# A decoder block on one core: 14 of 22 input-projection slabs by Strassen's seven products in a first phase

## Chip, core and metric

The kernel runs on one core of a Trainium2 chip. The metric is the device time of one execution in microseconds (us). Shown are the median of three runs and one further execution that was profiled.

## What is computed

The reference is one decoder block for 1024 tokens of width 1024: a norm, one input projection whose columns feed a gated linear attention (GLA), a retention and two merging gates, an output projection, and a mixture of 32 experts. All matrices are float32. Cut to what matters here:

```
u    = rmsnorm(x)                                # 1024 x 1024
proj = u @ w_in                                  # 1024 x 11280
gq, gk, gv, gg, gdown, rq, rk, rv, rg, mga, mgb = split(proj)
#512 512 1024 1024 16 1024 1024 2048 2048 1024 1024 columns
o_gla = rmsnorm(gla(gq, gk, gv, decay(gdown))) * silu(gg)
o_ret = groupnorm(retention(rotary(rq), rotary(rk), rv)) * silu(rg)
merged = sigmoid(mga) * (o_gla @ w_br_gla) + sigmoid(mgb) * (o_ret @ w_br_ret)
h = x + merged @ w_out
out = rmsnorm(h + moe(rmsnorm(h)))
```

Without the 16 columns of gdown the projection is 22 slabs of 512 columns: gq 1, gk 1, gv 2, gg 2, rq 2, rk 2, rv 4, rg 4, mga 2, mgb 2.

## The kernel before

**Arithmetic.** A float32 operand is split in two parts, hi and lo (`split`, L139: ScalarE casts to hi, VectorE subtracts to get lo). A product takes three matmuls, hi·hi, hi·lo, lo·hi (`Acc.add`, L154 to L157); each brings its own 128x128 stationary operand. Loading a weight slab of 1 MB and splitting it is `load_w` (L159): one DMA on SP's queue, two casts and two subtractions of 128x1024. Raw slabs have two buffers (`wraw`), split slabs two (`wsp`), and PSUM has eight banks.

**Order.** The tokens are done in two halves of 512, `Half(0)` and then `Half(1)`, and each half reads and splits all of w_in. `feat` (L323) makes 128 output columns as rows of a bank: 8 blocks of k by 3 matmuls, 24 in all, weights stationary and 512 tokens moving. `toks` (L331) makes 4 banks of 128 tokens by 512 columns: 96 matmuls for 1024 k, tokens stationary and 512 weight columns moving. So a 512-column slab costs 96 matmuls of 128x512 per half either way.

A half's program is a hand-written list (`seq`, `middle`, L1010 to L1130): norm and transposes of x (`start_x`, L304, `turn_x`), the decay's input, the gates mga and mgb (`gate`, L341, stored in DRAM), then GLA in two pairs of heads: `gq`, `gk`, `gv`, `gg`, the scores (`gs`), and four chunks (`gc`) that hand on a state. `gla_exact` (`gx`, L486) is a branch that is not taken here. After it come the norm of the GLA output (`gn`, L545), its transposes (`gt`, L559) and its projection (`gy`). The retention follows, head by head: `rk`, `rq` (two `feat` and a rotary on VectorE, L620), `rv`, `rg` (`toks`), `rkt`, scores (`rs`, L653), state (`rst`), output (`ro`, L724), its transposes (`rt`, L752) and its projection (`ry`, L764). The part of the list for head h with p = h - 1 reads

```
do(half, f"rk{h}", f"ro{p}", f"rq{h}", f"rt{p}", f"rv{h}0", f"rv{h}1", f"ry{p}0", f"ry{p}1")
```

so that the two `toks` calls of rv stand between the transposes of the previous head and its projection. The compiler layer turns the list into a fixed order for each engine; it may put an instruction that is ready ahead of one that isn't, with the list's order as priority, but it does not move work across the branch of `gx`. In the run each engine works its own order strictly.

The expert stage begins at about 1633 us and is untouched.

Of the kernel before, what the change touches and what calls it, by code (L numbers as in the profile page):

```python
# [28 lines left out]
SEQ = 1024  # L29
# [15 lines left out]
SPARE = 32  # L45
# [45 lines left out]
def hybrid_block(tc, a, out, dbg=None):  # L91
# [13 lines left out]
    sm_d = [tc.dram_tile([128, 8, HALF], F32, name=f"sm{i}_d") for i in range(2)]  # L105
# [13 lines left out]
    rsm = top.enter_context(tc.tile_pool(name="rsm", bufs=1))  # L119
# [39 lines left out]
    def load_w(src, kt, n, swap=False):  # L159

        raw = wraw.tile([128, kt, n], F32, name="w_raw", tag="w_raw")
        SP.dma_start(raw, src)
        if swap:
# [15 lines left out]
    upool = top.enter_context(tc.tile_pool(name="upool", bufs=4))  # L179
    mixers = contextlib.ExitStack()  # L180
    trig = mixers.enter_context(tc.tile_pool(name="trig", bufs=1))
    slots = mixers.enter_context(tc.tile_pool(name="slots", bufs=NSLOT))
    mixs = mixers.enter_context(tc.tile_pool(name="mixs", bufs=2))

    def slot(shape=(128, 512), dt=F32):
        return slots.tile(list(shape), dt, name="slot", tag="slot")

    x0 = [[slot(), slot()] for t in range(4)]
# [44 lines left out]

    s_gla = consts.tile([128, 4, 256], F32, name="s_gla")
    E_all = consts.tile([128, 2, 8, 32], F32, name="E_all")
    rk_all = consts.tile([128, 8, 2], F32, name="rk_all")

    rows_v = consts.tile([128, 8, 2, 2], F32, name="rows_v")
    DVE.tensor_copy(rows_v[:, :, :, 0], desth)
    DVE.tensor_copy(rows_v[:, :, :, 1], destl)  # L240
    wts_v = consts.tile([128, 8, 2, 3], BF16, name="wts_v")
    rows_b = consts.tile([128, 8, 2, 2, 32], BF16, name="rows_b")
    wts_b = consts.tile([128, 8, 2, 3, 32], BF16, name="wts_b")
    avs = consts.tile([128, 8, 2, CAP], BF16, name="avs")
# [20 lines left out]
    class Half:  # L265
# [8 lines left out]
        def load_x(self):  # L274
            if self.half == 0:
                self.xn = x0
                return
# [53 lines left out]
        def toks(self, w, part, accs):  # L331

            if part == 0:
                accs[:] = [Acc(bank(), 8) for t in range(4)]
            for t in range(4):
                for k in range(4):
                    s = slice(128 * t, 128 * t + 128)
                    accs[t].add(self.uh[4 * part + k][:, s], self.ul[4 * part + k][:, s], w[0][:, k, :], w[1][:, k, :])


        def gate(self, w, i, c, keep=False):  # L341
            for j in range(2):
                ps = self.feat(w, 128 * j)
                s = slot()
# [3 lines left out]
                else:  # L348
                    SP.dma_start(sm_d[i][:, 2 * c + j, :], s)
# [55 lines left out]
        def gla_q(self, w, pair):  # L405
            self.qt = []
            for j in range(2):
                ps = self.feat(w, 128 * j)
                q = self.ep[2 * pair + j]
                DVE.scalar_tensor_tensor(q, ps, 128.0 ** -0.5, q, op0=OP.mult, op1=OP.mult)  # L410
                self.qt.append(q)

        def gla_k(self, w, pair):
            self.kt = []
            for j in range(2):
                ps = self.feat(w, 128 * j)
                k = self.en[2 * pair + j]
                DVE.tensor_mul(k, ps, k)
                self.kt.append(k)

        def gla_v(self, w, part):
            if part == 0:
                self.accs = []
            self.toks(w, part, self.accs)
            if part == 1:
                self.v = []
                for t in range(4):
                    s = slot((128, 2, 256))
                    ACT.copy(s.rearrange("p j d -> p (j d)"), self.accs[t].ps)
                    self.v.append(s)  # L430

        def gla_g(self, w, part, pair):
            if part == 0:
                self.accs = []
            self.toks(w, part, self.accs)
            if part == 1:
                self.gg = getattr(self, "gg", {})
                for t in range(4):
                    s = slot((128, 2, 256))
                    ACT.activation(s.rearrange("p j d -> p (j d)"), self.accs[t].ps, AF.Silu)  # L440
                    self.gg[pair, t] = s

        def gla_scores(self):
            self.sc, self.kk = [], []
            for j in range(2):
                q, k = self.qt[j], self.kt[j]
# [13 lines left out]
        def gla_chunk(self, c, pair):  # L460
# [7 lines left out]
            for j in range(2):  # L468
                h = 2 * pair + j
                vc = self.v[c][:, j, :]  # L470
                PE.matmul(po[:, j, :], self.sc[j][:, c, :], vc, start=True, stop=first)
                if not first:
                    PE.matmul(po[:, j, :], self.qt[j][:, 128 * c:128 * c + 128], s_gla[:, h, :], start=False, stop=True)
# [98 lines left out]
        def gla_y(self, w, c):  # L572

            for j in range(2):
                s = slot()
                SP.dma_start(s, sm_d[0][:, 2 * c + j, :])
# [43 lines left out]
        def rotary(self, w):  # L620

            pe, po = self.feat(w, 0), self.feat(w, 128)
# [11 lines left out]
        def ret_k(self, w):  # L634
            self.kr = self.rotary(w)

        def ret_q(self, w):
# [38 lines left out]
        def ret_v(self, w, part, h):  # L676
            if part == 0:
                self.accs = []
            self.toks(w, part, self.accs)
            if part == 1:  # L680
                self.vh = [slot(dt=F32R) for _ in range(4)]
                self.vl = [slot(dt=F32R) for _ in range(4)]
                for t in range(4):
                    split(self.vh[t], self.vl[t], self.accs[t].ps, gneg[:, h, t:t + 1])

        def ret_g(self, w, part, h):
            if part == 0:
                self.accs = []
            self.toks(w, part, self.accs)
            if part == 1:  # L690
                self.sg = [slot() for _ in range(4)]
                for t in range(4):
                    ACT.activation(self.sg[t], self.accs[t].ps, AF.Silu)
# [94 lines left out]
        def load_m(self):  # L788
            self.mg, self.mh, self.ml = [], [], []
            for f in range(8):  # L790
# [3 lines left out]
                if g is None:  # L794
                    g = slot()
                    SP.dma_start(g, sm_d[1][:, f, :])
# [153 lines left out]


# [24 lines left out]
    gix = consts.tile([CAP, 32], I32, name="gix")  # L976
    swt = consts.tile([CAP, 32], F32, name="swt")

# [20 lines left out]
    prog = []  # L999

    def add(fn, *args, spec=None):
        prog.append((spec, fn, args))
# [4 lines left out]
    def s512(w, off, part):  # L1007
        return (w[:, 4 * part:4 * part + 4, off:off + 512], 4, 512, False)

    def seq(z):  # L1010
# [7 lines left out]
        put("start", z.start_x)  # L1018
# [7 lines left out]
        for i, off in enumerate((OFF_MA, OFF_MB)):  # L1026
            for c in range(4):
                put(f"gate{4 * i + c}", z.gate, i, c, z.half == 1 and 4 * i + c == 7, spec=s256(off + 256 * c))
        for p in range(2):
            put(f"gq{p}", z.gla_q, p, spec=s256(OFF_GQ + 256 * p))  # L1030
            put(f"gk{p}", z.gla_k, p, spec=s256(OFF_GK + 256 * p))
            for part in range(2):
                put(f"gv{p}", z.gla_v, part, spec=s512(w_in, OFF_GV + 512 * p, part))
                put(f"gg{p}", z.gla_g, part, p, spec=s512(w_in, OFF_GG + 512 * p, part))
            put(f"gs{p}", z.gla_scores)
# [9 lines left out]
        for h in range(4):  # L1045
            put(f"rk{h}", z.ret_k, spec=s256(OFF_RK + 256 * h, True))
            put(f"rq{h}", z.ret_q, spec=s256(OFF_RQ + 256 * h, True))
            for part in range(2):
                put(f"rv{h}{part}", z.ret_v, part, h, spec=s512(w_in, OFF_RV + 512 * h, part))
                put(f"rg{h}{part}", z.ret_g, part, h, spec=s512(w_in, OFF_RG + 512 * h, part))  # L1050
# [23 lines left out]
    def middle(half, mix):  # L1074

        def at(n):
# [3 lines left out]
        do(half, "gq0", "gk0", "gv0")  # L1080
        at("gs0")
        do(half, "gs0", "gc00", "gg0", "gc01", "gc02", "gc03", "gq1", "gk1", "gv1", "gs1",
           "gc10", "gg1", "gc11", "gc12", "gc13", "gx", "gn0", "rk0", "gn1")
        at("gt0")
        do(half, "gt0", "gt1", "gy0", "gy1", "gy2", "gy3", "rq0")
        for h in range(4):
            p = h - 1
            if h:
                do(half, f"rk{h}", f"ro{p}", f"rq{h}", f"rt{p}", f"rv{h}0", f"rv{h}1", f"ry{p}0", f"ry{p}1")
                if half == 0:  # L1090
                    do(half, f"rkt{h}")
            elif half == 0:
                do(half, "rv00", "rkt0", "rv01")
# [313 lines left out]
```

## Time and profile before

| | us |
|---|---|
| median of 3 runs | 2281.86 (2277.16 to 2282.0) |
| profiled execution, its time | 2281.08 |
| its span, first to last instruction | 2279.1 |
| TensorE matmul busy | 2177.4 (96%) |
| VectorE busy | 1311.9 (58%) |
| ScalarE busy | 1083.0 (48%) |

In the views an instruction is named by line, engine, operation and `out<-in`; `bank<-w_hi,uh` is a matmul into PSUM with w_hi moving and uh stationary. PE is TensorE, PEld its weight loads, DVE VectorE, ACT ScalarE. Matmuls overlap in their pipeline, so what one costs is the distance between starts and not its duration.

### The profile page before, as it was taken

Reading aid. Unit: us, or ns where it says so; the run is one execution under the profiler, and the core shown is the slowest. Engines: PE = TensorE matmul, PEld = TensorE weight load, DVE = VectorE, ACT = ScalarE, POOL = GpSimd, SP = SyncE. Lnnn points to the kernel's source line nnn. Section 1 sums busy time; section 2 is a strip of 40 time slices with the busy share of each in tenths; the row PEclk is TensorE's granted clock in tenths of the full one; section 3 lists DMA queues with packets and bytes.
Section 4 is the critical chain, followed back from the end, with each engine's and each line's share of the span. In section 5 each row is a group of like instructions: output and inputs, shape, how many; then the busy total and the mean of one; then the engine's idle time right before and its main releaser. Section 6 shows DMA issues by size and latency. Waiting matters only on the chain. (4 is left out here: it accounts for less than half of the span.)

```text
span 2279.1 us, 25815 instructions
## 1 busy us (share of the span) xinstructions
PE 2177.4 (96%) x9950; PEld 1765.5 (77%) x9951; DVE 1311.9 (58%) x2015; ACT 1083.0 (48%) x1504; POOL 145.5 (6%) x116
## 2 busy tenths in 40 slices
PE   6999999999999999999999999999599999999993
PEld 5888788888888888887888888878467777777772
DVE  5522354525356628334445354535588888888886
ACT  5522433333334437323233332333377888888885
POOL 1000000000000011000000000001311111111102
PEclk9999999999999999999999999999799999999996
DMA  5432242222223544222422222237489999998995
GB/s 166 144 115 74 85 155 95 84 93 83 99 77 111 202 146 164 95 74 77 175 96 70 93 76 100 74 120 277 174 315 324 368 370 370 371 369 312 369 364 201
DMA packets 157953, 406.16 MB, mean 178 GB/s; under 512 B 13887, under 2 KB 65119, under 8 KB 133488
## 3 DMA queue, kind: packets, MB, share of 16 engines
q1 hardware_dynamic: 149088, 387.01, 47.4%
q0 software_dynamic: 8720, 17.28, 3.2%
q8 instruction: 83, 1.36, 0.2%
q14 instruction: 62, 0.51, 0.1%
HBM read 372.97 MB, written 44.04 MB: 183 GB/s over the span
## 5 line engine op out<-in xcount | busy, mean ns | idle before, releaser
L142 ACT CAST w_hi<-w_raw 128x1024 fp32r<-128x1024 f32 (+1 forms) x244 | 247.8, 1052 | 559.8 <-PE bank L156 488.8
L143 DVE TENSOR_TENSOR w_lo<-w_raw,w_hi 128x1024 fp32r<-128x1024 f32 (+1 forms) x244 | 293.3, 1225 | 365.6 <-ACT w_hi L142 347.1
L143 DVE TENSOR_TENSOR m_lo<-m_raw,m_hi 128x1024 fp32r<-128x1024 f32 x380 | 445.1, 1219 | 66.7 <-ACT m_hi L142 64.4
L142 ACT CAST m_hi<-m_raw 128x1024 fp32r<-128x1024 f32 x380 | 381.8, 1050 | 68.0 <-PE bank L156 63.8
L156 PE MATMUL bank<-w_hi,uh 128*128 128x512 f32 x768 | 300.7, 392 | 0.0
L156 PE MATMUL bank<-w_lo,uh 128*128 128x512 f32 x768 | 299.3, 390 | 0.0
L156 PE MATMUL bank<-w_hi,ul 128*128 128x512 f32 x768 | 299.2, 390 | 0.0
L156 PE MATMUL bank<-uh,w_hi 128*128 128x512 f32 x656 | 261.5, 399 | 7.9 <-ACT junk L256 4.0
L156 PE MATMUL bank<-ul,w_hi 128*128 128x512 f32 x656 | 259.9, 396 | 0.0
L156 PE MATMUL bank<-uh,w_lo 128*128 128x512 f32 x656 | 259.3, 395 | 0.0
L156 PE MATMUL bank<-slot,w_hi 128*128 128x512 f32 x768 | 237.0, 390 | 1.1 <-DVE slot L146 0.9
L156 PE MATMUL bank<-m_lo,xh 128*112 128x512 f32 x512 | 206.8, 404 | 0.7 <-DVE m_lo L143 0.2
L156 PE MATMUL bank<-m_hi,xh 128*112 128x512 f32 x512 | 204.8, 400 | 1.9 <-ACT xh L142 1.6
L156 PE MATMUL bank<-m_hi,xl 128*112 128x512 f32 x512 | 202.6, 396 | 0.0
L156 PEld LDWEIGHTS bank<-slot,w_hi 128*128 128x128 f32 x768 | 144.0, 188 | 32.0 <-DVE slot L146 1.7
L156 PEld LDWEIGHTS bank<-w_hi,ul 128*128 128x128 f32 x768 | 144.2, 188 | 30.1
L156 PEld LDWEIGHTS bank<-w_hi,uh 128*128 128x128 f32 x768 | 144.3, 188 | 29.4
L156 PEld LDWEIGHTS bank<-w_lo,uh 128*128 128x128 f32 x768 | 144.3, 188 | 29.3
L156 PEld LDWEIGHTS bank<-uh,w_hi 128*128 128x128 f32 x656 | 125.9, 192 | 38.2 <-ACT junk L256 4.4
L156 PE MATMUL bank<-slot,w_lo 128*128 128x512 f32 x384 | 149.1, 390 | 0.0
L156 PEld LDWEIGHTS bank<-uh,w_lo 128*128 128x128 f32 x656 | 125.6, 191 | 26.7 <-issue 0.3
L156 PEld LDWEIGHTS bank<-ul,w_hi 128*128 128x128 f32 x656 | 125.9, 192 | 25.9
(264 smaller groups left out, 2890.7 us busy)
## 6 DMA issues: line engine op xcount, KB each, us to landing
w_raw<-in_w_in_dram SPq DMA_DIRECT2D x88, 1024.0 KB, 4.7
m_raw<-in_expert_w_down_dram SPq DMA_DIRECT2D x64, 1024.0 KB, 12.9
m_raw<-in_expert_w_gate_dram SPq DMA_DIRECT2D x63, 1024.0 KB, 13.3
m_raw<-in_expert_w_up_dram SPq DMA_DIRECT2D x63, 1024.0 KB, 12.7
w_raw<-in_w_branch_ret_dram SPq DMA_DIRECT2D x16, 1024.0 KB, 4.8
slot<-in_x_dram SPq DMA_DIRECT2D x32, 256.0 KB, 6.0
w_raw<-in_w_branch_gla_dram SPq DMA_DIRECT2D x8, 1024.0 KB, 4.9
w_raw<-in_w_out_dram SPq DMA_DIRECT2D x8, 1024.0 KB, 5.8
```

Source lines behind the costliest of these rows:

```text
L142: ACT.copy(hi, src)
L143: DVE.tensor_sub(lo, src, hi.bitcast(F32))
L156: PE.matmul(self.ps, l, r, start=self.i == 0, stop=self.i == 3 * self.n - 1)
```

## The change

A class `Front` runs ahead of the two halves. It takes 14 slabs (mga 2, gv 2, gg 2, rv 4, rg 4) for all 1024 tokens at once. With tokens, k and columns each cut in two, a slab is a 2x2 by 2x2 block product of eight products of 512 tokens by 512 k by 256 columns; the Winograd form of Strassen's scheme needs seven, with sums of the left blocks (S1 to S4, made once), sums of the right blocks (per slab) and sums of the results. The products run in the order a11, s2, a12, s3, s1, a22, s4 (left blocks and sums); `pair` makes and splits their right sums, two at a time, a pair ahead. `turn` transposes the second half's x and makes S1 and S2, `third` and `fourth` make S3 and S4 with two VectorE sums and a split for each of four k blocks. Results go to DRAM (silu and sigmoid applied), and the halves load them back where they computed them before. The weights of these slabs are read once and not twice. The other eight slabs stay in the halves; their calls are cut in two (`gq0a`, `gq0b`, ...). The order lists are rewritten.

```diff
+        def product(self, feat, left, right):
+            (lh, ll), (rh, rl) = left, right
+            banks = [bank(), bank()]
+            for j in range(2):
+                for t in range(1 if feat else 2):
+                    acc = Acc(banks[j] if feat else banks[j][:, 256 * t:256 * t + 256], 4)
+                    for k in range(4):
+                        if feat:
+                            s = slice(128 * j, 128 * j + 128)
+                            acc.add(rh[:, k, s], rl[:, k, s], lh[k], ll[k])
+                        else:
+                            s = slice(256 * j + 128 * t, 256 * j + 128 * t + 128)
+                            acc.add(lh[k][:, s], ll[k][:, s], rh[:, k, :], rl[:, k, :])
+            return banks
+        def pair(self, z, i):
+            (b11, b12), (b21, b22) = ((r[:, :, :256], r[:, :, 256:]) for r in z["raw"])
+            if i == 0:
+                z["x"] = x = fl.tile([128, 4, 256], F32, name="x_raw")
+                DVE.tensor_sub(x, b22, b12)
+                DVE.tensor_sub(b12, b12, b11)
+                r = self.rights(2)
+                split(*r[0], b11)
+                DVE.tensor_add(b11, b11, x)
+                split(*r[1], b11)
+            elif i == 1:
+                r = self.rights(2)
+                split(*r[0], b21)
+                split(*r[1], z["x"])
...
+        def slab(self, z, r, then):
+            nxt = then(0)
+            ps = self.product(feat, self.a11, r[0])
+            p1 = [fs.tile([128, HALF], F32, name="fs", tag="fs") for j in range(2)]
+            for j in range(2):
+                ACT.copy(p1[j], ps[j])
+            ps = self.product(feat, self.s2, r[1])
+            u2 = [self.room() for j in range(2)]
+            for j in range(2):
+                DVE.tensor_add(u2[j], ps[j], p1[j])
...
+        def turn(self, k):
...
+            ACT.activation(r3, ps[0], AF.Copy, scale=nmix[:, k:k + 1])
+            DVE.scalar_tensor_tensor(r1, ps[1], nmix[:, k + 4:k + 5], r3, op0=OP.mult, op1=OP.add)
+            split(self.a22[0][k], self.a22[1][k], ps[1], nmix[:, k + 4:k + 5])
+            DVE.tensor_sub(r2, r1, h11)
+            DVE.tensor_sub(r2, r2, l11)
+            split(self.s2[0][k], self.s2[1][k], r2)
+            split(self.s1[0][k], self.s1[1][k], r1)
...
+    H[0].start_x()
+    H[0].gate(w, 1, 0, early=True)
+    for t in range(4):
+        H[1].norm_x(t)
+    for k in range(4):
+        fr.turn(k)
+    H[0].gate(w, 1, 1, early=True)
+    r0 = fr.pair(z0, 0)
+    for k in range(4):
+        fr.third(k)
+    for k in range(4):
+        fr.fourth(k)
+    fr.run(pieces, r0, z0)
+        def rows_of(self, src, c0):
+            res = [slot() for t in range(4)]
+            for t in range(4):
+                r0 = self.tok0 + 128 * t
+                SP.dma_start(res[t], src[r0:r0 + 128, c0:c0 + 512])
+            return res
-        do(half, "gs0", "gc00", "gg0", "gc01", "gc02", "gc03", "gq1", "gk1", "gv1", "gs1",
-           "gc10", "gg1", "gc11", "gc12", "gc13", "gx", "gn0", "rk0", "gn1")
+        do(half, "gs0", "gq1a", "gc00", "gq1b", "gc01", "gv1", "gk1a", "gc02", "gk1b", "gc03", "gs1", "gg0",
+           "rk0a", "gc10", "rk0b", "gc11", "rq0a", "gc12", "rq0b", "gc13", "gg1", "gx", "gn0", "gn1")
         at("gt0")
-        do(half, "gt0", "gt1", "gy0", "gy1", "gy2", "gy3", "rq0")
+        do(half, "gt0", "gt1", "rv0", "gy0", "gy1", "gy2", "gy3")
-                do(half, f"rk{h}", f"ro{p}", f"rq{h}", f"rt{p}", f"rv{h}0", f"rv{h}1", f"ry{p}0", f"ry{p}1")
+                do(half, f"rk{h}a", f"rk{h}b", f"ro{p}", f"rv{h}", f"rq{h}a", f"rq{h}b", f"rt{p}", f"ry{p}0", f"ry{p}1")
...
+            do(half, f"rvs{h}", f"rs{h}", f"rg{h}")
...
-    middle(0, {"gt0": [(0, ["gate7"])], "rg30": [(1, ["x"])], "rg31": [(1, ["norm0", "norm1"])], "rst3": [(1, ["norm2", "norm3"])]})
+    middle(0, {"gt0": [(0, ["gate3"])], "rst3": [(1, ["x", "norm0", "norm1", "norm2", "norm3"])]})
...
-    middle(1, {"gs0": [(0, ["rd"])], "gt0": [(1, ["gate6"])]})
-    do(1, "ro3", "gate7", "rt3", "lm", "ry30", "ry31", "lh", "wo00", "wo01", "th0")
+    middle(1, {"gt0": [(0, ["rd"])]})
+    do(1, "ro3", "gate3", "rt3", "lm", "ry30", "ry31", "lh", "wo00", "wo01", "th0")
```

In the new lists `gv`, `gg`, `rv` and `rg` are loads alone, and `rvs` splits the loaded rv.

## Rows read from the trace of the kernel before

**Rows 1.** The page: busy time, then TensorE and its granted clock in 40 slices.

```profile
PE 2177.4 (96%) x9950; PEld 1765.5 (77%) x9951; DVE 1311.9 (58%) x2015; ACT 1083.0 (48%) x1504; POOL 145.5 (6%) x116
...
PE   6999999999999999999999999999599999999993
...
PEclk9999999999999999999999999999799999999996
```

**Rows 2.** Who TensorE waited for: us in total, times, longest us.

```profile
PE bank L294 <- DVE slot L291: 17.2, 5, 11.4
...
PE bank L156 <- ACT junk L256: 4.0, 1, 4.0
```

**Rows 3.** Stretches of 50 us: busy TensorE, loads, VectorE, ScalarE, GpSimd, clock, DMA share.

```profile
200.00:250.00 50.00, 50.00 (x234) 41.68 (x233) 13.94 (x16) 11.81 (x15) 0.00 (x0) 1.00 0.25 85
...
1050.00:1100.00 50.00, 45.30 (x205) 36.78 (x204) 30.41 (x72) 24.87 (x55) 0.00 (x0) 0.93 0.37 124
```

**Rows 4.** TensorE in order of time: start, us; 512-wide matmuls, first and last of 44.

```profile
386.15 0.39 PE L156 MATMUL bank<-w_hi,uh 128*128 128x512 f32 x1
...
395.90 0.39 PE L156 MATMUL bank<-w_lo,uh 128*128 128x512 f32 x1
```

**Rows 5.** The same, the 256-wide matmuls of one call of `rs`, merged.

```profile
382.66 1.59 PE L156 MATMUL bank<-slot 128*128 128x256 f32 x12
```

**Rows 6.** Groups by line and shape: count, busy us, mean ns of one; TensorE, loads.

```profile
L156 PE MATMUL bank<-slot 128*128 128x256 f32 x96 | 12.7, 282 | 0.0
...
L156 PEld LDWEIGHTS bank<-w_hi,uh 128*128 128x128 f32 x768 | 144.3, 188 | 29.4
```

**Rows 7.** Groups by line and shape on VectorE and ScalarE.

```profile
L143 DVE TENSOR_TENSOR w_lo<-w_raw,w_hi 128x1024 fp32r<-128x1024 f32 x240 | 290.7, 1233 | 365.6 <-ACT w_hi L142 347.1 <-PE bank L647 8.2 <-PE bank L828 7.9
...
L777 DVE TENSOR_TENSOR yb<-yb,bank 128x512 f32<-128x512 f32 x48 | 32.7, 684 | 46.3 <-PE bank L156 46.3
...
L142 ACT CAST w_hi<-w_raw 128x1024 fp32r<-128x1024 f32 x240 | 245.5, 1059 | 558.8 <-PE bank L156 488.3 <-issue 67.3 <-ACT slot L345 1.6
```

**Rows 8.** DMA issues: KB each, median us from issue to landing.

```profile
w_raw<-in_w_in_dram SPq DMA_DIRECT2D x88, 1024.0 KB, 4.7
```

**Rows 9.** The start in order of time: TensorE and VectorE.

```profile
25.54 0.80 PE L156 MATMUL bank<-uh,w_hi 128*128 128x512 f32 x1 [0.22 <-DVE ul L146]
...
22.80 0.88 DVE L291 TENSOR_SCALAR slot<-slot,rstd 128x512 f32<-128x512 f32 x2
...
24.74 5.35 DVE L146 SCALAR_TENSOR_TENSOR ul<-bank,nmix,uh 128x512 fp32r<-128x512 f32 x8
```

**Rows 10.** TensorE in order of time: the 32 transposes of the second half's x.

```profile
735.87 3.65 PE L294 MATMUL bank<-ct,slot 128*128 128x128 f32 x32
```

**Rows 11.** After the branch of `gx`, second half: TensorE, then VectorE's first norm.

```profile
1058.63 0.77 PE L156 MATMUL bank<-uh,w_hi 128*128 128x512 f32 x1 [4.01 <-ACT junk L256]
...
1063.24 0.58 PE L156 MATMUL bank<-ul,w_hi 128*128 128x512 f32 x1
1063.65 0.39 PE L156 MATMUL bank<-uh,w_lo 128*128 128x512 f32 x1
...
1068.03 3.26 DVE L556 SCALAR_TENSOR_TENSOR slot<-slot,rstd 128x256 f32<-128x256 f32 x8
```

**Rows 12.** TensorE: one whole call of `rs`, and one of `rkt`.

```profile
380.23 4.01 PE L156 MATMUL bank<-slot 128*128 128x512 f32 x24
...
368.46 1.03 PE L647 MATMUL bank<-ct,slot 128*128 128x128 f32 x8
```

**Rows 13.** The transposes `rt` of one head, and the splits that follow them.

```profile
439.88 1.98 PE L758 MATMUL bank<-ct,slot 128*128 128x128 f32 x16
...
440.07 0.69 DVE L627 TENSOR_TENSOR slot<-bank,sin_t 128x512 f32<-128x512 f32 x1 [2.29 <-PE bank L156]
...
441.41 2.35 DVE L143 TENSOR_TENSOR w_lo<-w_raw,w_hi 128x1024 fp32r<-128x1024 f32 x2
...
447.63 2.72 DVE L146 SCALAR_TENSOR_TENSOR slot<-bank,rnw,slot 128x512 fp32r<-128x512 f32 x4
```

More of the change, by code (lines that the diff above doesn't have):

```diff
@@ L104, in hybrid_block @@
     st_d = tc.dram_tile([4, 128, 2, 512], F32, name="st_d")
-    sm_d = [tc.dram_tile([128, 8, HALF], F32, name=f"sm{i}_d") for i in range(2)]
+    sm_d = [tc.dram_tile([128, 8, SEQ], F32, name=f"sm{i}_d") for i in range(2)]
+    gv_d = tc.dram_tile([SEQ, 1024], F32, name="gv_d")
+    gg_d = tc.dram_tile([SEQ, 1024], F32, name="gg_d")
+    rv_d = tc.dram_tile([SEQ, 2048], F32, name="rv_d")
+    rg_d = tc.dram_tile([SEQ, 2048], F32, name="rg_d")
     ma_d = tc.dram_tile([128, 8, HALF], F32, name="ma_d")
@@ L162, in load_w, with split_w @@
         SP.dma_start(raw, src)
+        return split_w(raw, kt, n, swap)
+    def split_w(raw, kt, n, swap=False):
         if swap:
@@ L178, in hybrid_block, with left_sum @@
     ypool = top.enter_context(tc.tile_pool(name="ypool", bufs=8))
[L179 to L188, printed above, removed]
+    front = contextlib.ExitStack()
+    fl = front.enter_context(tc.tile_pool(name="fl", bufs=1))
+    fs = front.enter_context(tc.tile_pool(name="fs", bufs=4))
+    def left_sum(name):
+        return [fl.tile([128, 4, HALF], F32R, name=f"{name}{p}") for p in ("h", "l")]
+    s1, s2, a22 = left_sum("s1"), left_sum("s2"), left_sum("a22")
+    rows = contextlib.ExitStack()
+    fx = rows.enter_context(tc.tile_pool(name="fx", bufs=1))
+    x0, x1 = ([[fx.tile([128, HALF], F32, name=f"x{h}{t}{c}") for c in range(2)] for t in range(4)] for h in range(2))
     for c in range(2):
@@ L329, in feat, with gate @@
             return ps
[L331 to L341, printed above, removed]
+        def gate(self, w, i, c, keep=False, early=False):
             for j in range(2):
                 ps = self.feat(w, 128 * j)
-                s = slot()
+                s = fs.tile([128, HALF], F32, name="fs", tag="fs") if early else slot()
                 ACT.activation(s, ps, AF.Sigmoid)
@@ L421, in gla_v @@
[L421 to L441, printed above, removed]
@@ L443, in gla_scores, with gla_q, gla_k @@
-        def gla_scores(self):
+        def gla_q(self, w, pair, j):
+            if w is not None:
+                self.w = w
+            ps = self.feat(self.w, 128 * j)
+            q = self.ep[2 * pair + j]
+            DVE.scalar_tensor_tensor(q, ps, 128.0 ** -0.5, q, op0=OP.mult, op1=OP.mult)
+        def gla_k(self, w, pair, j):
+            if w is not None:
+                self.w = w
+            ps = self.feat(self.w, 128 * j)
+            k = self.en[2 * pair + j]
+            DVE.tensor_mul(k, ps, k)
@@ new lines, in rows_of, with gla_v, gla_g @@
+        def rows_of(self, src, c0):
[4 more added lines that the diff above has]
+            return res
+        def gla_v(self, pair):
+            self.v = getattr(self, "v", {})
+            self.v[pair] = [z.rearrange("p (j d) -> p j d", j=2) for z in self.rows_of(gv_d, 512 * pair)]
+        def gla_g(self, pair):
+            self.gg = getattr(self, "gg", {})
+            for t, z in enumerate(self.rows_of(gg_d, 512 * pair)):
+                self.gg[pair, t] = z.rearrange("p (j d) -> p j d", j=2)
@@ L469, in gla_chunk @@
                 h = 2 * pair + j
-                vc = self.v[c][:, j, :]
+                vc = self.v[pair][c][:, j, :]
                 PE.matmul(po[:, j, :], self.sc[j][:, c, :], vc, start=True, stop=first)
                 if not first:
-                    PE.matmul(po[:, j, :], self.qt[j][:, 128 * c:128 * c + 128], s_gla[:, h, :], start=False, stop=True)
+                    PE.matmul(po[:, j, :], self.ep[h][:, 128 * c:128 * c + 128], s_gla[:, h, :], start=False, stop=True)
                 if not last:
@@ L674, in ret_scores, with ret_v, ret_vs, ret_g @@
                 self.pl.append(lo)
[L676 to L693, printed above, removed]
+        def ret_v(self, h):
+            self.vr = self.rows_of(rv_d, 512 * h)
+        def ret_vs(self, h):
+            self.vh, self.vl = [], []
+            for t in range(4):
+                hi, lo = slot(dt=F32R), slot(dt=F32R)
+                split(hi, lo, self.vr[t], gneg[:, h, t:t + 1])
+                self.vh.append(hi)
+                self.vl.append(lo)
+        def ret_g(self, h):
+            self.sg = self.rows_of(rg_d, 512 * h)
         def ret_state(self, h):
@@ L998, in hybrid_block @@
     H = [Half(0), Half(1)]
-    prog = []
-    def add(fn, *args, spec=None):
-        prog.append((spec, fn, args))
+    H[0].xn = x0
     def s256(off, swap=False):
@@ L1008, in s512 @@
         return (w[:, 4 * part:4 * part + 4, off:off + 512], 4, 512, False)
+    early = []
+    for c in range(2):
+        raw = wraw.tile([128, 8, 256], F32, name="w_raw", tag="w_raw")
+        SP.dma_start(raw, s256(OFF_MB + 256 * c)[0])
+        early.append(raw)
+    for t in range(4):
+        for c in range(2):
+            SP.dma_start(x1[t][c], x_t[:, 4 + t, 512 * c:512 * c + 512])
+    H[0].start_x()
+    pieces = [(True, AF.Sigmoid, sm_d[0], OFF_MA + 512 * i, 512 * i) for i in range(2)]
@@ new lines, in hybrid_block @@
+    for dst, fn, off, n in ((gv_d, None, OFF_GV, 2), (gg_d, AF.Silu, OFF_GG, 2), (rv_d, None, OFF_RV, 4), (rg_d, AF.Silu, OFF_RG, 4)):
+        pieces += [(False, fn, dst, off + 512 * i, 512 * i) for i in range(n)]
+    fr = Front(H[0].uh, H[0].ul)
+    w = split_w(early[0], 8, 256)
+    H[0].gate(w, 1, 0, early=True)
+    H[1].xn = x1
+    for t in range(4):
+        H[1].norm_x(t)
+    w = split_w(early[1], 8, 256)
+    for k in range(4):
+        fr.turn(k)
+    H[0].gate(w, 1, 1, early=True)
@@ new lines, in hybrid_block @@
+    z0 = dict(raw=[fr.load(pieces[0][3], kh) for kh in range(2)])
+    r0 = fr.pair(z0, 0)
+    rows.close()
+    fl2 = front.enter_context(tc.tile_pool(name="fl2", bufs=1))
+    fr.s3, fr.s4 = (fr.by_k([fl2.tile([128, 4, HALF], F32R, name=f"{n}{p}") for p in ("h", "l")]) for n in ("s3", "s4"))
+    for k in range(4):
[3 more added lines that the diff above has]
+    fr.run(pieces, r0, z0)
+    front.close()
+    keep = top.enter_context(tc.tile_pool(name="keep", bufs=1))
@@ new lines, in hybrid_block, with slot @@
+    rsm = top.enter_context(tc.tile_pool(name="rsm", bufs=1))
+    mixers = contextlib.ExitStack()
+    trig = mixers.enter_context(tc.tile_pool(name="trig", bufs=1))
+    slots = mixers.enter_context(tc.tile_pool(name="slots", bufs=NSLOT))
+    mixs = mixers.enter_context(tc.tile_pool(name="mixs", bufs=2))
+    def slot(shape=(128, 512), dt=F32):
+        return slots.tile(list(shape), dt, name="slot", tag="slot")
+    s_gla = keep.tile([128, 4, 256], F32, name="s_gla")
+    E_all = keep.tile([128, 2, 8, 32], F32, name="E_all")
@@ L1010, in seq, with add @@
+    DVE.memset(base, 0.0)
+    flag_i = keep.tile([1, 2], I32, name="flag_i")
+    gix = keep.tile([CAP, 32], I32, name="gix")
+    swt = keep.tile([CAP, 32], F32, name="swt")
+    prog = []
+    def add(fn, *args, spec=None):
+        prog.append((spec, fn, args))
     def seq(z):
@@ L1025, in seq @@
             put("r" + n, getattr(z, "route_" + n))
-        for i, off in enumerate((OFF_MA, OFF_MB)):
-            for c in range(4):
-                put(f"gate{4 * i + c}", z.gate, i, c, z.half == 1 and 4 * i + c == 7, spec=s256(off + 256 * c))
+        for c in range(4):
+            put(f"gate{c}", z.gate, 1, c, z.half == 1 and c == 3, spec=s256(OFF_MB + 256 * c))
         for p in range(2):
[L1030 to L1035, printed above, removed]
+            put(f"gq{p}a", z.gla_q, p, 0, spec=s256(OFF_GQ + 256 * p))
+            put(f"gq{p}b", z.gla_q, None, p, 1)
+            put(f"gk{p}a", z.gla_k, p, 0, spec=s256(OFF_GK + 256 * p))
+            put(f"gk{p}b", z.gla_k, None, p, 1)
+            put(f"gv{p}", z.gla_v, p)
+            put(f"gg{p}", z.gla_g, p)
+            put(f"gs{p}", z.gla_scores, p)
             for c in range(4):
@@ L1045, in seq @@
         for h in range(4):
[L1046 to L1050, printed above, removed]
+            put(f"rk{h}a", z.ret_k, spec=s256(OFF_RK + 256 * h, True))
+            put(f"rk{h}b", z.ret_k)
+            put(f"rq{h}a", z.ret_q, spec=s256(OFF_RQ + 256 * h, True))
+            put(f"rq{h}b", z.ret_q)
+            put(f"rv{h}", z.ret_v, h)
+            put(f"rvs{h}", z.ret_vs, h)
+            put(f"rg{h}", z.ret_g, h)
             put(f"rkt{h}", z.ret_kturn)
@@ L1111, in hybrid_block @@
     do(1, "gate1")
-    do(0, "wo00", "wo01")
-    do(1, "gate2")
-    do(0, "th0", "wo10", "wo11")
-    do(1, "da", "gate3")
-    do(0, "th1")
-    do(1, "db", "gate4")
+    do(0, "wo00", "wo01", "wo10", "wo11")
+    do(1, "da", "gv0", "gate2")
+    do(0, "th0", "th1")
+    do(1, "db")
     do(0, "ra")
```

192 lines of the change are left out of this document (134 added, 58 removed).

## The prediction

> **What bounds the kernel now.** The page's busy times come first: TensorE 96%, VectorE 58%, ScalarE 48% of the span [rows 1]. The 40 slices show where the missing 4% lies: the first slice, the step from the projections to the experts (slice 29) and the end; in between TensorE is full at the full clock [rows 1]. A busy TensorE may still be waiting on something, so the waits come next: over the whole span the largest is 17.2 us at the start, on the norms of x, and the next is one wait of 4.0 us [rows 2]. The stretches say the same from the other side: between 200 and 250 us TensorE is busy for all 50 us, VectorE for 13.9, ScalarE for 11.8, and DMA has a share of 0.25 [rows 3]. So until 1633 us the time is the number of matmuls times their distance, and other engines matter only where TensorE waits for them.
>
> The distance is read from starts. Forty-three steps from 386.15 to 395.90 us give 226.7 ns for a 512-wide matmul [rows 4]. Twelve 256-wide ones take 1.59 us together, the last of them 282 ns, so (1.59 - 0.28) / 11 = 118.8 ns each, with a fresh stationary operand every time [rows 5, 6]. Twice 118.8 is 237.6: a narrow matmul costs 5% more per column.
>
> **The change part by part.**
>
> *Products.* Before, a slab costs 2 x 96 matmuls of 226.7 ns = 43.5 us over both halves. After, the two gate slabs take 7 x 24 = 168 of them, 38.1 us, and save 10.9 us together. The twelve token slabs take 7 x 48 = 336 narrow ones, 336 x 118.8 ns = 39.9 us, and save 3.6 us each, 43.3 us. Sum: **-54.2 us**. Strassen's eighth would be 76 us; the rest goes on the narrow form.
>
> *Right sums, splits and result sums inside the phase.* Per slab VectorE has 7 splits and 4 sums of 128x1024 at 1.23 us and 14 result sums of 0.68 us, 23 us; ScalarE has 7 casts of 1.06 us and some ten small ones, 14 us [rows 7]. Both lie beside 38 to 40 us of matmuls, and the pairs are split a pair ahead. The tightest place is the slab's end: the next slab's first right block can be cast only when a22 has released its buffer, and needs cast plus split, 2.3 us, and up to 1.4 us of result sums, while s4 covers it with 5.5 to 5.7 us. I take nothing; with that cover gone it would be about 2 us x 13.
>
> *DMA.* Weights of the 14 slabs are read once (28 MB less), results are written and read back (29 MB each way). A slab's 4 MB stand beside 39 us, and 1 MB lands in 4.7 us [rows 8]. The loads wait on SP behind the stores of results; those are ready before the next raw buffer is free. The reloads are issued well ahead of use. I take nothing. Late next, if at all, would be `gg1`, whose slots come free last.
>
> *The start.* Matmuls begin at 25.5 us as before: the first gate's weights can be split in the pauses of the norms. Behind that, VectorE owes much before TensorE can go on. From 30.1 us, when the splits of u end [rows 9]: one weight slab 2.4, four norms about 11 (13 small steps and two scalings each, 0.88 for the scalings [rows 9]), `turn` 4 x 6 x 0.68 = 16, the first pair 6.1, `third` and `fourth` 24 x 0.68 = 16, the second pair's first split 1.2: 53 us, so until 83 us. TensorE has two gates (96 x 226.7 ns = 21.8 us), 32 transposes (3.7 us [rows 10]) and two products (10.9 us) to set against it, 36 us, until 62. The gap is 21 us if VectorE works strictly in the list's order, and 13 if the second pair goes ahead of `fourth`, 8 us long. I take **+18 us**, nearer the strict order.
>
> *After `gx`.* Before, the next matmul follows 4.0 us after the last, and the chain to the first normed GLA rows ends at 1068.03 + 3.26 = 1071.3, 12.7 us after that matmul's start [rows 11]. What covers it now is `toks` work, `rk0` and a gate. After the change the first half has `gate3` (10.9 us) and the scores of head 0 (4.0 us [rows 12]) and loses nothing. The second half has only the scores: 12.7 - 4.0 = 8.7, so **+9 us**; from 6 us, if more can be put there, to 13 us.
>
> *Between `rt` and `ry`.* Here 96 matmuls of `rv`, 21.8 us, go away. The transposes end at 439.88 + 1.98 = 441.9 us, and the first of the four splits on VectorE that `ry` needs ends near 447.63 + 0.74 = 448.4: 6.5 us, because the rotary of `rq` and a weight slab stand before it on VectorE [rows 13]. Both stay there (`ry`'s second slab takes the place of `rv`'s). The place recurs for three heads in each half. TensorE may take `rs` (4.0 us) and in the first half `rkt` (1.0 us) meanwhile [rows 12], as both stand next in the list. I take 2.5 and 1.5 us, **+12 us** for the six. The ends: 1.1 us each, if the rotary were out of the way too, and 6.5 us each.
>
> *Smaller edges.* The changeover from the phase to the halves (a chain of cast and split), and `rt3` before `ry30` in the second half: +2 us each, **+4 us**; from 0 to 10. The cut of calls in two adds no instruction. The new layout of pools is taken at nothing, as it must only hold the same buffers.
>
> Sum: -54.2 + 18 + 9 + 12 + 4 = **-11 us**. The profiled execution took 2281.1 us, 0.8 under the median, so 2270 in the profile's terms and 2271 as a median.
>
> **A rule against it.** Twelve matmuls in a row with a fresh stationary operand start 118.8 ns apart although one load is 188 ns long, so loads run beside matmuls and beside each other [rows 5, 6]. The Trainium skill, "TensorE: Matmul & The Clock Gate", section "The mechanism", states that a weight load overlaps a running matmul only where their row groups differ, which none does here. By that rule the narrow form would pay 4032 loads where the wide one paid 2304; 1728 more at the trace's 188 ns are an estimate of +325 us on the sum above, 2596 us. The trace contradicts it over a run of twelve; a milder form of it is rival C.
>
> **Rivals.**
>
> *A, the waits stay open: slower.* For A speaks that each engine's order is fixed beforehand, and that in the trace ScalarE and VectorE take `rt`'s splits 5 us after the banks are full [rows 13]; `rs` needs the same rotary, so it may come no earlier than `ry`. Then the six places cost 6.5 us each, 39. A gap also costs clock: after the 4.0 us wait matmuls start 0.43 us apart, 1.2 GHz, from 1058.6 to 1063.6 us, some 12 of them at 0.2 us extra, 2.4 us, and that stretch has a granted clock of 0.93 [rows 3, 11]. Six gaps at 2.4 us add 14. With start 21, `gx` 12 and edges 4: -54.2 + 90 = +36, **2318 us**. With the other terms as I took them it decides from 54 - 31 = 23 us over six places, 4 us each.
>
> *B, the gaps fill.* The compiler's order finds work for all: start 13, `gx` 6, six places at 1.1 us, no edges: -54.2 + 26 = -28, **2254 us**. For it speaks that the order before, with as many chains, leaves TensorE full in the middle, as from 200 to 250 us [rows 3], and that its largest single wait there is the branch's 4.0 us [rows 2].
>
> *C, weight loads set the pace.* 4032 narrow matmuls at 188 instead of 118.8 ns: +279 us, **2550 us**. Only a longer run than twelve could show it.
>
> That the phase saves no matmul time is excluded by the counts unless C holds.
>
> **How the numbers follow.** Forecast 0.40, A 0.27, B 0.30, C 0.03. The forecast's own range, with its terms at their nearer bounds, is about 2258 to 2284. The range from 2242 to 2316 holds B with some room below (half the start's bound), the forecast and about half of A; C and the worse half of A are left out. About 0.2% is what a measurement of this kernel can tell, 4.6 us. B and three quarters of the forecast are faster, most of the rest of it the same, A and C slower: 0.59, 0.12, 0.29.
>
> **What would show it.** In the changed profile: narrow matmuls 118 to 120 ns apart and some 40 us per token slab, without waits at slab ends; the phase ending near 25.5 + 21.8 + 3.7 + 18 + 555 = 624 us; one or two waits before 85 us that add to some 18 us, released by VectorE; one wait of 9 us for the normed GLA rows in the second half; six waits between `rt` and `ry` of 1 to 3 us. Six of 6 us with a lower clock behind each would mean A. It would be wrong in kind if the narrow matmuls kept another distance, or VectorE were behind inside the phase.

## The result and the profile after: slower by 2.6%

The changed kernel takes 2337.45 us (median of four executions, 2337.18 to 2344.56), the kernel before 2281.69 us beside it: ratio 1.0257, 95% interval 1.0233 to 1.028. The prediction was 2271 us, from 2242 to 2316; its sign was wrong and its range missed. The execution with the profile is the longest of the four, 2344.56 us with a span of 2342.7 us, so sums of its rows come out some 7 us above the median.

The page of the changed kernel, busy time and TensorE with its granted clock in 40 slices:

```profile
PE 2161.1 (92%) x11662; PEld 1829.4 (78%) x11663; DVE 1522.9 (65%) x2361; ACT 1086.3 (46%) x1532; POOL 146.2 (6%) x116
...
PE   6899999999999999989997889979788999999993
...
PEclk9999999999999999999989899989889999999997
```

Beside [rows 1] TensorE is busy for 16 us less, far from the 54 us that the products were to save, and the span is 64 us longer. Counted from 0, slices 2 to 10, which lie in the new phase, are full; from slice 17 on TensorE, and from slice 20 its clock too, have holes where the kernel before has none. They have names in the waits of TensorE (us in total, times, longest us), to be read against [rows 2]:

```profile
PE bank L161 <- ACT slot L150: 34.6, 7, 5.7
PE bank L542 <- DVE slot L532: 24.3, 6, 18.5
...
PE bank L161 <- DVE w_lo L148: 13.9, 2, 9.5
PE bank L161 <- ACT slot L147: 9.7, 2, 9.6
...
PE bank L286 <- DVE slot L283: 5.0, 3, 4.4
```

In the order of these lines they are: the six places between `rt` and `ry`, 5.7 us each; the norms behind `gx`; the start and a gate; `rs` of head 3 before its `ro`; the turn of the second half's x.

The stretches, as in [rows 3]: one in the phase, one with one of the six places, and the whole way to the first expert's rows:

```profile
200.00:250.00 50.00, 50.00 (x419) 50.00 (x418) 27.83 (x33) 11.90 (x13) 0.00 (x0) 1.00 0.35 117
...
1380.00:1430.00 50.00, 44.28 (x204) 36.88 (x203) 22.25 (x44) 21.11 (x35) 0.00 (x0) 0.93 0.24 80
...
0.00:1708.82 1708.82, 1572.80 (x8975) 1382.10 (x8976) 983.53 (x1782) 591.54 (x919) 48.46 (x53) 0.95 0.37 126
```

The same way in the kernel before:

```profile
0.00:1643.28 1643.28, 1588.29 (x7262) 1317.25 (x7264) 772.55 (x1436) 588.06 (x891) 50.86 (x53) 0.98 0.34 117
```

The expert stage behind it is as long as before (2342.7 - 1708.8 = 633.9 us against 2279.1 - 1643.3 = 635.8), so all of the loss lies ahead of it: 65.5 us. TensorE's idle time there grows from 1643.28 - 1588.29 = 55.0 to 1708.82 - 1572.80 = 136.0 us, by 81.0. Its busy time falls by only 15.5 us and its mean clock from 0.98 to 0.95.

The phase itself did what it promised. The first and the last narrow matmul in TensorE's order of time:

```profile
144.67 0.28 PE L161 MATMUL bank<-w_hi,uh 128*128 128x256 f32 x1
...
628.38 0.28 PE L161 MATMUL bank<-w_hi,s4l 128*128 128x256 f32 x1
```

There are 4032 of them, so (628.38 - 144.67) / 4031 = 120.0 ns each, without a wait. Groups of such matmuls and their loads, by shape:

```profile
L161 PE MATMUL bank<-w_hi,uh 128*128 128x256 f32 x384 | 108.7, 283 | 0.0
...
L161 PEld LDWEIGHTS bank<-w_hi,uh 128*128 128x128 f32 x384 | 73.7, 192 | 0.0
```

A load is 192 ns long and a new one is needed every 120.0 ns: loads overlap matmuls and one another all the way, which takes away the ground for rival C. The rule of the Trainium skill that was set against the change ("TensorE: Matmul & The Clock Gate", "The mechanism") does not hold here in the form stated, over 4032 matmuls instead of twelve.

With 120.0 ns a token slab takes 336 x 0.120 = 40.3 us and saves 3.2; the products save 10.9 + 12 x 3.2 = 49.3 us. All of it and 56 us more is lost elsewhere. One of the six places, on TensorE, VectorE and ScalarE:

```profile
852.38 1.97 PE L733 MATMUL bank<-ct,slot 128*128 128x128 f32 x16
860.08 1.65 PE L161 MATMUL bank<-slot,w_hi 128*128 128x512 f32 x3 [5.74 <-ACT slot L150]
861.53 0.63 PE L161 MATMUL bank<-slot,w_lo 128*128 128x512 f32 x1
861.95 1.05 PE L161 MATMUL bank<-slot,w_hi 128*128 128x512 f32 x2
...
866.16 0.39 PE L161 MATMUL bank<-slot,w_lo 128*128 128x512 f32 x1
...
858.10 0.69 DVE L608 TENSOR_TENSOR slot<-slot 128x512 f32<-128x512 f32 x1
859.47 0.69 DVE L148 TENSOR_TENSOR slot<-slot 128x512 fp32r<-128x512 f32 x1 [0.68 <-ACT slot L147]
860.08 2.72 DVE L151 SCALAR_TENSOR_TENSOR slot<-bank,rnw,slot 128x512 fp32r<-128x512 f32 x4
...
858.82 0.62 ACT L147 CAST slot<-slot 128x512 fp32r<-128x512 f32 x1 [3.55 <-DVE slot L608]
859.35 2.42 ACT L150 ACTIVATE slot<-bank,rnw 128x512 fp32r<-128x512 f32 x4
```

The transposes end at 854.35. VectorE and ScalarE are still on the rotary of `rq` (L608, then its split L147 and L148) and come to the splits of `rt` (L150, L151) when that is done; only then has `ry` an operand. So 5.74 us of idle TensorE, and behind it matmuls 0.43 us apart, which is 1.2 GHz. Fourteen of them start from 860.08 us until the next at 866.16: 6.1 us, where 14 x 226.7 ns would be 3.2. So this wait cost 2.9 us beyond its own length.

### The profile page after: what moved, and what is told of

Its sections match the earlier page's. It is cut to its first block, busy times and chain, and to the rows that moved or that the text cites. A ratio compares the mean times of both kernels' runs of the same rounds, so it can differ in the third digit from the quotient of the medians.

```text
span 2342.7 us, 30241 instructions
## 1 busy us (share of the span) xinstructions
PE 2161.1 (92%) x11662; PEld 1829.4 (78%) x11663; DVE 1522.9 (65%) x2361; ACT 1086.3 (46%) x1532; POOL 146.2 (6%) x116
## 5 line engine op out<-in xcount | busy, mean ns | idle before, releaser
L147 ACT CAST w_hi<-w_raw 128x1024 fp32r<-128x1024 f32 (+1 forms) x216 | 221.7, 1053 | 583.9 <-PE bank L161 449.7
L148 DVE TENSOR_TENSOR m_lo<-m_raw,m_hi 128x1024 fp32r<-128x1024 f32 x380 | 445.0, 1219 | 65.7 <-ACT m_hi L147 64.9
L147 ACT CAST m_hi<-m_raw 128x1024 fp32r<-128x1024 f32 x380 | 381.8, 1050 | 66.5 <-PE bank L161 64.3
L148 DVE TENSOR_TENSOR w_lo<-w_raw,w_hi 128x1024 fp32r<-128x1024 f32 (+1 forms) x216 | 259.5, 1216 | 115.9 <-ACT w_hi L147 115.7
L161 PE MATMUL bank<-slot,w_hi 128*128 128x512 f32 x768 | 248.2, 406 | 34.6 <-ACT slot L150 34.6
L161 PE MATMUL bank<-uh,w_hi 128*128 128x512 f32 x560 | 227.4, 406 | 7.1 <-DVE w_lo L148 4.5
L161 PE MATMUL bank<-uh,w_lo 128*128 128x512 f32 x560 | 223.2, 399 | 9.5 <-DVE w_lo L148 9.5
L161 PE MATMUL bank<-ul,w_hi 128*128 128x512 f32 x560 | 223.7, 399 | 0.0
L161 PEld LDWEIGHTS bank<-slot,w_hi 128*128 128x128 f32 x768 | 150.6, 197 | 69.4 <-ACT slot L150 36.3
L161 PE MATMUL bank<-slot 128*128 128x512 f32 (+2 forms) x624 | 136.0, 375 | 10.3 <-ACT slot L147 9.7
L161 PEld LDWEIGHTS bank<-slot 128*128 128x128 f32 x624 | 110.8, 190 | 32.4 <-ACT slot L147 10.5
L161 PEld LDWEIGHTS bank<-m_lo,xh 128*112 128x112 f32 x512 | 90.3, 176 | 35.5 <-DVE m_lo L148 9.5
L161 PEld LDWEIGHTS bank<-m_hi,xh 128*112 128x112 f32 x512 | 90.4, 177 | 31.2 <-ACT xh L147 2.0
L161 PEld LDWEIGHTS bank<-m_hi,xl 128*112 128x112 f32 x512 | 90.0, 176 | 26.2 <-DVE xl L148 0.6
```

Source lines behind the costliest of these rows:

```text
L147: ACT.copy(hi, src)
L148: DVE.tensor_sub(lo, src, hi.bitcast(F32))
L161: PE.matmul(self.ps, l, r, start=self.i == 0, stop=self.i == 3 * self.n - 1)
```

## Experiments

The theory: the phase saves its 49 us, and the rest is waits of TensorE, each where a call of `rv`, `rg`, `gv` or `gg` used to stand, and each costing its length and slow matmuls behind it. The rivals: the phase is paced by something else; the slow matmuls cost nothing by themselves; a wait that is closed only opens the next.

**The kernel before, with the cover of the six places taken away** (`b1_uncover`). If the theory holds, its middle must get the same holes without any Strassen:

```diff
- do(half, f"rk{h}", f"ro{p}", f"rq{h}", f"rt{p}", f"rv{h}0", f"rv{h}1", f"ry{p}0", f"ry{p}1")
+ do(half, f"rk{h}", f"ro{p}", f"rq{h}", f"rt{p}", f"ry{p}0", f"ry{p}1", f"rv{h}0", f"rv{h}1")
```

> The kernel before (2281.7 us), nothing of the first phase, with rv moved behind ry in the order of each head, so that rt and ry stand together as in the changed kernel. Theory (cover alone): six waits of 6.5 us open, 39 us, and 2.4 us of slow clock behind each, 14 us: 2335. Without a price of the clock 2321. Rival (the compiler's order finds other work, as the sum of the prediction had it): 2282 to 2295.

Measured 2327.19 us, ratio 1.0217 (1.02 to 1.0234). Its wait and its whole stretch:

```profile
PE bank L156 <- ACT slot L145: 34.6, 7, 5.8
```

```profile
0.00:1685.90 1685.90, 1594.57 (x7262) 1320.42 (x7264) 773.31 (x1436) 587.52 (x891) 50.95 (x53) 0.97 0.34 114
```

The same 34.6 us as in the changed kernel. Idle time is 91.3 us against 55.0, and busy time for the same matmuls 6.3 us more. So two calls of `rv` had hidden 5.8 us at each place while they cost their 21.8 us anyway, and uncovering them costs more than the idle time alone: 42 us by the spans, 48 by the medians, for waits of 34.6. The time lies between the theory's 2335 us and its 2321 without a price of the clock: beside 36.3 us more of idle time, what the clock adds is 6 us by the spans and some 11 by the medians.

**The six waits of the changed kernel closed by order** (`e1_rt`): `ro` between the halves of rk, `rt` between those of rq, so that 5.4 us of matmuls lie behind each.

```diff
- f"rk{h}a", f"rk{h}b", f"ro{p}", f"rv{h}", f"rq{h}a", f"rq{h}b", f"rt{p}", f"ry{p}0", f"ry{p}1")
+ f"rk{h}a", f"ro{p}", f"rk{h}b", f"rv{h}", f"rq{h}a", f"rt{p}", f"rq{h}b", f"ry{p}0", f"ry{p}1")
```

> The changed kernel (2337 us) with one line of the order altered: ro of the previous head goes between the two halves of rk, and rt between the two halves of rq, so that 24 matmuls (5.4 us) stand between rt and ry. Theory (uncovered waits in the halves, each with a slow clock behind it): the six waits of 5.7 us go, and with them 2.4 us of slow matmuls each: 6 x 8.1 = -49 us, less some us for a tighter ro to rt, so 2288 to 2300. Rival (the wait only moves, to rt, which now has 10.9 us behind ro): 2325 to 2340. Rival (the loss sits in the first phase or in the DRAM trips): 2337.

Measured 2310.86 us, ratio 1.0134 (1.0107 to 1.0161): 27 us gained, short of the 37 to 49 that were expected. The wait on L150 is gone, and this one has grown:

```profile
PE bank L161 <- ACT slot L147: 24.9, 4, 10.1
```

It is `ro`, which now comes sooner after `rs` and waits for the splits of the scores, at all four heads of the second half. A wait that is closed can open the next: that rival holds in part.

**The six waits filled with matmuls of no use** (`e4_junk`), which leaves every chain as it is, so that what can change is the clock:

```diff
+            if h < 3:
+                ps = bank()
+                for i in range(20):
+                    PE.matmul(ps, self.uh[i % 8][:, :128], self.uh[i % 8], start=i == 0, stop=i == 19)
```

> The changed kernel with 20 extra 512-wide matmuls of no use (4.5 us) put behind the transposes rt of heads 0 to 2 in each half, into the six waits of 5.7 us; the extra product is not read by anything. Theory (a wait costs its length and then matmuls at 1.2 GHz behind it): the work that matters comes no earlier, but TensorE stays at 2.4 GHz; the kernel before with such waits opened showed 12 us of slow matmuls for six waits, so 2322 to 2328 us. Rival (only the length of the waits costs): nothing is gained, 2335 to 2345 us, a little more where the extra matmuls run past the wait.

Measured 2326.52 us (2322.01 to 2334.33), ratio 1.0212 (1.0179 to 1.0245). TensorE at the place shown above:

```profile
850.47 1.97 PE L733 MATMUL bank<-ct,slot 128*128 128x128 f32 x16
852.19 4.83 PE L741 MATMUL bank<-uh 128*128 128x512 f32 x20
858.18 1.43 PE L161 MATMUL bank<-slot,w_hi 128*128 128x512 f32 x5 [1.16 <-ACT slot L150]
859.44 0.39 PE L161 MATMUL bank<-slot,w_lo 128*128 128x512 f32 x1
```

The useful matmuls start as late as before behind the transposes (5.7 us after these end), but now 0.23 us apart from the second on. 120 more matmuls make the kernel 11 us faster (no execution of the two overlaps), 1.8 us for each wait. The slow matmuls cost by themselves.

**rq0 behind the branch** (`e2_gx`): both halves of rq of head 0 go from ahead of `gx` to between and behind the norms.

```diff
- "rk0a", "gc10", "rk0b", "gc11", "rq0a", "gc12", "rq0b", "gc13", "gg1", "gx", "gn0", "gn1")
+ "rk0a", "gc10", "gc11", "rk0b", "gc12", "gc13", "gg1", "gx", "rq0a", "gn0", "rq0b", "gn1")
```

> The changed kernel with rq0 moved behind the branch gx, between the two GLA norms, in both halves (10.9 us of matmuls). Theory (the second half's 18.5 + 3.9 us of waiting behind its last chunk is missing cover): about 11 us less waiting in the second half, and a branch that need not wait for the rotary of rq0, so -11 to -16 us, 2321 to 2326. Rival (the chunks now lose their own cover, or the wait moves to gy): 2333 to 2342.

Measured 2329.28 us, ratio 1.0221 (1.0204 to 1.0238). The waits there:

```profile
PE bank L161 <- PEq L467: 9.0, 2, 4.9
PE bank L449 <- DVE s_gla L459: 6.0, 4, 2.0
PE bank L542 <- DVE slot L532: 5.9, 2, 5.6
```

The 24.3 us on L542 are 5.9; the branch itself keeps 4 to 5 us in each half, and the chunks, now with less between them, wait on their state. Some 8 us are gained, less than the 11 to 16 that were expected.

**fourth behind the second pair** (`e3_start`):

```diff
-    for k in range(4):
-        fr.fourth(k)
...
             nxt = then(0)
+            if not self.done4:
+                self.done4 = True
+                for k in range(4):
+                    self.fourth(k)
```

> The changed kernel with the fourth left sum made after the second pair of right sums of the first slab. Theory (the 9.5 us wait at 70 us is VectorE working strictly in the list's order): up to 8 us less, with the slow clock behind it 9, 2328 to 2331. Rival (VectorE is behind anyway, and the wait comes at s4): 2335 to 2339.

Measured 2332.58 us, ratio 1.0243 (1.0224 to 1.0261). The wait of 9.5 us became these two:

```profile
PE bank L161 <- ACT w_hi L147: 2.4, 1, 2.4
...
PE bank L161 <- DVE w_lo L148: 2.2, 1, 2.2
```

The medians differ by some 5 us, less than the 6 to 9 that were expected; one of the four executions (2339.14 us) lies among those of the changed kernel, so the gain is the least certain of these.

**The phase with an eighth product** (`e7_eight`), the test of the phase's pace: the a11 product done twice, its second result not used.

```diff
+            self.product(feat, self.a11, r[0])
             r, nxt = nxt, then(1)
             ps = self.product(feat, self.a12, r[0])
```

> The changed kernel with an eighth product in each of the 14 slabs: the a11 product is done twice, and the second result is not used. Theory (in the phase the time is the matmuls times their distance): 12 slabs x 48 x 120.0 ns + 2 slabs x 24 x 226.7 ns = 80 us more, 2412 to 2422 us. Rival (VectorE, at 65% of the span, or the right sums set part of the phase's pace): the extra product goes partly into time that TensorE has, below 2400 us.

Measured 2414.42 us, ratio 1.0586 (1.0563 to 1.0609): 77 us above the changed kernel, within what matmuls at their distance give; the 9.5 us wait at the start fell to 4.2 us, which is more than the 3 us that are missing to 80. So in the phase the time is the products at their distance, and what the eighth would have cost is saved.

**The gains together.** Next, the new `rs`-to-`ro` waits were covered too (`e5b_rtrs`): in the second half `rvs` and `rs` go between the two slabs of `ry`.

```diff
- f"rq{h}b", f"ry{p}0", f"ry{p}1")
+ f"rq{h}b", f"ry{p}0")
+ do(half, *([f"rvs{h}", f"rs{h}"] if half else []), f"ry{p}1")
```

> As e1_rt, and in the second half rvs and rs of head h stand between the two slabs of ry, so that 10.9 us of matmuls lie between the scores and the ro that needs their splits. e1_rt was 2310.9 us with 14.8 us of new waits at three rs-to-ro places and 10.1 at the last. Theory (what is lost are waits, and each can be covered): 25 us of waits and 5 to 8 us of slow matmuls less, 2278 to 2288 us. Rival (the waits only move on, since ScalarE and VectorE have too much queued in the second half): 2300 to 2312 us.

Measured 2289.37 us, ratio 1.0043 (1.0029 to 1.0058): 21 us under `e1_rt`, 1 us above the range of the theory; the wait on L147 fell from 24.9 to 7.0 us.

With the edits of `e2_gx` and `e3_start` added (`e5c_nog2`):

> As e5b_rtrs, with the edits of e2_gx (rq0 behind the branch) and e3_start (fourth behind the second pair) added. Those gave 8 us and 5 us alone. Theory (the waits are separate and add up): 13 us under e5b_rtrs, 2265 to 2276 us, under the kernel before. Rival (a gain in one place is lost in the next, as with the waits of e1_rt): within 5 us of e5b_rtrs.

Measured 2278.24 us, ratio 0.9993 (0.9983 to 1.0003). They bring 11 of the 13 us that they brought alone, 2 us short of the range of the theory: separate waits nearly add up.

With gate2 of the second half moved behind the branch as well (`e5_all`):

```diff
- do(1, "da", "gv0", "gate2")
+ do(1, "da", "gv0")
...
- middle(1, {"gt0": [(0, ["rd"])]})
+ middle(1, {"gt0": [(0, ["rd"]), (1, ["gate2"])]})
```

> As e5c_nog2, with gate2 of the second half moved from the decay's chain to behind the branch gx, where 14 us of waits were left in e2_gx. Theory: 10.9 us of matmuls fill most of them, and the output projection and transposes of the first half cover the decay's chain in its old place: 8 to 12 us under e5c_nog2, 2255 to 2267 us, faster than both kernels. Rival: the decay's chain opens instead (its VectorE scans and ScalarE functions have only some 10 us of matmuls beside them): within 4 us of e5c_nog2, or above.

Measured 2281.89 us, ratio 1.0 (0.999 to 1.0011), no gain. The wait on L542 is gone, and where gate2 had stood this one came:

```profile
PE bank L812 <- ACT slot L805: 8.8, 6, 7.3
```

That is not the decay's chain, as the rival had it, but the first half's router, which waits for its transposed rows: gate2 had covered it. A matmul that fills one hole is missing where it came from.

Last, order alone (`e6_more`): both norms ahead of rq0 in the list, and in the second half `ro` of head 0 behind both halves of rk1.

```diff
- "gx", "rq0a", "gn0", "rq0b", "gn1")
+ "gx", "gn0", "gn1", "rq0a", "rq0b")
...
- f"rk{h}a", f"ro{p}", f"rk{h}b", f"rv{h}",
+ f"rk{h}a", *([f"rk{h}b", f"ro{p}"] if half and h == 1 else [f"ro{p}", f"rk{h}b"]), f"rv{h}",
```

> As e5c_nog2 (2278.2 us), with two of its open waits gone after: in the second half both norms of the GLA output stand ahead of rq0 in the list, so that VectorE does not hold the second norm (5.6 us of wait) behind the rotary; and ro of head 0 stands behind both halves of rk1, which puts 5.4 us more between its scores and it (4.0 us of wait). Theory (each open wait is worth its length and its slow matmuls, in any order): 6 to 10 us less, 2268 to 2273 us, under the kernel before. Rival (the rotary, now later, holds the scores or the next split): 2276 to 2281 us, no difference from e5c_nog2.

Measured 2273.72 us (median of 12, 2266.05 to 2276.78), ratio 0.997 (0.9958 to 0.9982): below the theory's gain by a microsecond or two, and faster than both kernels. Its stretches:

```profile
0.00:1639.30 1639.30, 1555.59 (x8974) 1366.95 (x8975) 984.59 (x1782) 590.09 (x919) 47.37 (x53) 0.97 0.39 131
1380.00:1430.00 50.00, 49.82 (x232) 41.13 (x231) 33.48 (x59) 16.52 (x24) 0.00 (x0) 1.00 0.26 84
```

With the work of the phase unchanged, idle time is 83.7 us instead of 136.0 and busy time 17 us less, so 69.5 us came back from the order of the lists in the profiled executions, and 64 by the medians. No run gives the kernel before a new order, so what order alone could do for it stays open; it had 55.0 us of idle time.

## Why the prediction was wrong

The sum by its own steps, the profiled execution's numbers against the ones before, up to the first expert's rows:

| step | forecast | measured |
|---|---|---|
| products | -54.2 | -49.3 |
| start | +18 | +17.3 |
| after `gx` | +9 | +21.1 |
| between `rt` and `ry` | +12 | +34.4 |
| smaller edges | +4 | +13.1 |
| slower matmuls and transposes behind the waits | none | +29 |
| sum | -11 | +65.5 |

The middle rows are idle time read from TensorE's order of time; the start is 12.9 us of idle and 4.4 us for 32 transposes that only the phase needs. The last row is a remainder and no view shows it as such: the busy time fell by 15.5 us where -49.3 + 4.4 was due.

**Right.** The products came out within 5 us: the distance over a long run is 120.0 ns and not 118.8. Right sums, splits and DMA cost nothing, as forecast: no wait at slab ends. The phase ended at 628.7 us against 624. The largest of the start's three waits, 9.5 us, has VectorE as its releaser, as forecast; but the three (1.9, 1.8 and 9.5) add to 13 us and not to 18. The term comes out at 17.3 only with the 4.4 us of transposes, which the prediction had set against the gap and never counted as new work: that agreement is luck.

**The step that failed: "TensorE may take `rs` and in the first half `rkt` meanwhile".** The length of each hole had been worked out well from [rows 13], 6.5 us, measured 5.7. But of it 4 to 5 us were then taken off for work that could not come: `rs` needs the rotary of `rq`, whose last split ends at 860.16 us (859.47 + 0.69) in the rows above, just when `ry`'s operand is there too. What delays `ry` delays `rs` as well. The prediction said so itself under rival A and still kept the lower value as the likeliest. `rkt` was ready, but TensorE takes the list in order: the trace has it behind `ry`.

**After `gx`: the cover was not there.** The scores of head 0 were counted as 4.0 us of cover, but in the list `rs0` stands behind `gy`, and the first thing behind the branch in the second half is `gt0`, which needs the norms. And the chain was longer, as both halves of rq0 had been put ahead of the branch. TensorE, VectorE and ScalarE of the changed kernel:

```profile
1273.34 0.59 PE L449 MATMUL bank<-s_gla,slot 128*128 128x256 f32 x2
1292.39 3.87 PE L542 MATMUL bank<-ct,slot 128*128 128x128 f32 x16 [18.46 <-DVE slot L532]
...
1279.01 0.69 DVE L148 TENSOR_TENSOR slot<-slot 128x512 fp32r<-128x512 f32 x1 [0.68 <-ACT slot L147]
1289.39 0.17 DVE L527 TENSOR_SCALAR ss<-ss 128x8 f32<-128x8 f32 x1 [9.69 <-ACT junk L251]
...
1283.78 1.28 ACT L251 ACT_TABLE_LOAD   x1 [4.31 <-ACTq L467]
```

The last matmul ends at 1273.9; the rotary holds VectorE until 1279.7; only then is the branch passed, ScalarE begins at 1283.8 with the squares, and the transposes start at 1292.4: 18.5 us, then 3.9 for the second norm. Less the 4.0 us of before that is 18.4, and the first half adds 2.7.

**Edges that were not looked for.** Removing the calls of `rg` and `rv` also uncovered `rs` before `ro` of head 3 (9.6 us, before 3.1) and the turn of the second half's x (5.2 us); the changeover took 1.4.

**The price of the clock was in rival A alone.** There it was 14 us for six waits, worked out from [rows 3, 11]; the forecast had 39 us at the start, after `gx` and between `rt` and `ry`, and put no slow matmuls behind any of it, without a reason given. For the six, `e4_junk` takes back 11 us, and `b1_uncover` shows 6 to 11; in all it is some 29 us, as the remainder of the busy time in the profiled execution. How that spreads over the single waits is not shown.

Rival A named the mechanism and nearly the time: 2318 us. It fell short by the longer wait after `gx`, the edges, the slow matmuls behind the other waits and the 5 us that the products saved less. Its mark, "six of 6 us with a lower clock behind each", is what the rows show. Rival B did not come true in the kernel as written, but an order nearer to it exists: the last experiment has the same products and takes 2273.7 us, against B's 2254.

## What to carry to other kernels

In a kernel whose busiest engine is full, each block of work also hides something. Before a block is taken out, list for every place where it stood what the engine does next and which chain that must wait for; another piece of work is cover only if it does not wait for the same chain. Price each opened wait at its length plus the slow matmuls behind it, and rearrange the order together with the saving: here the saving alone gave +2.6%, and the same saving with a new order -0.3%.

## What was not expected of the hardware

- A 256-wide matmul starts 120.0 ns after the last and a 512-wide one 226.7 ns [rows 4]. The difference, 106.7 ns, is 256 columns at 2.4 GHz; so 13.3 ns are left over at either width, and that fixed part makes the narrow form 5.9% dearer per column. What it consists of no run shows, as every matmul brings a load at both widths.
- Useless matmuls in a wait made the kernel faster, by 1.8 us for 4.8 us of them at each place.
